# The second layer's modulation, summed over row blocks on VectorE

## The chip, the cores and the metric

The kernel runs on one core of a Trainium2 chip. The metric is the device time of one execution in microseconds, the median of several runs. A profile is one further execution, recorded by the hardware profiler.

## What is computed

The reference is a trunk of two layers over 512 latent tokens and 256 context tokens, 1024 wide. In each layer six vectors of 1024 numbers, the modulation, scale, shift and gate the tokens:

```
for l in range(DEPTH):                          # DEPTH = 2
    ctx_out = l < DEPTH - 1
    mod_l = (silu_c @ w_mod[l] + b_mod[l])      # for the latent tokens
    mod_c = (silu_cc @ w_mod[l] + b_mod[l])     # for the context tokens
    sh_m, sc_m, gt_m, sh_f, sc_f, gt_f = split(mod, 6)   # for l and for c
    hl = rmsnorm(xl, g_pre_mix) * (1 + sc_ml) + sh_ml    # hc likewise
    y_c, y_l = token_mixing(hc @ w_in, hl @ w_in, ...)   # S5, neighbourhood, GLA, windowed heads
    xl = xl + gt_ml * rmsnorm(y_l @ w_out, g_post_mix)
    hl = rmsnorm(xl, g_pre_ffn) * (1 + sc_fl) + sh_fl
    xl = xl + gt_fl * rmsnorm(conv_ffn(hl, w_up, conv_w, w_down), g_post_ffn)
    if ctx_out: the same two updates for the context tokens xc
return xl
```

`w_mod[l]` has 1024 rows and 6144 columns, so that one layer's modulation reads 25 MB for two vectors (one for each kind of token). In the last layer only `sh_m` and `sc_m` are needed for the context, since its other outputs are not.

## The kernel before, in words

Channels lie on partitions, 8 tiles of 128 (`KT = 8`), tokens along the free axis. Large products are made of three matmuls each (high and low parts of both operands, `split`, L243): ScalarE makes the high part of a weight tile or of an activation, VectorE the low one.

**The modulation.** `silu_c` (L166) leaves `cT`: for each of the 8 tiles of channels 32 columns, of which the first two are the two streams (latent and context) and the rest zero. A round of `mod_round` (L180) makes 2048 of the 6144 columns. It goes over 32 blocks of `w_mod`, 128 rows by 512 columns and 256 KB each, loaded by SP into three buffers of the tag `wm`. Each block is multiplied on TensorE by `cT` in four matmuls, one for each 128 columns, which write the four groups of 32 partitions of one PSUM tile `modp` and accumulate over the 8 tiles of channels; as the operands are float32, each matmul is two instructions, so a block is eight. At the end of a round VectorE copies the PSUM tile (`modrow`), TensorE turns it in four transposes (`modt`), and VectorE adds the bias and makes the factors that the layer uses. The first round of layer 0 is made by another function (`mod_first`, L1633).

**When a round is made.** Rounds are generators, one step a block. They wait in the list `later`, and `pump(n)` (L1296) takes n steps. In the mixing of a layer `gap` (L487) calls pump at each gap between units of attention, GLA or S5; in the feed-forward stage `ffn` (L1571) calls it once after each f from 2 on, with n = 4 (`KN['pump']`, L1582). Layer 0's mixing makes rounds 1 and 2 of layer 0; layer 0's feed-forward stage makes rounds 0 and 1 of layer 1 (`L1748`); layer 1's mixing makes round 2 of layer 1 (`mods`, L1374 and L1424), from the GLA stage on.

**The feed-forward stage.** There are 22 f, blocks of 128 hidden channels in groups of 6, 6, 6 and 4. For each f, `dense` (L434, its matmuls at L442) makes gate and value of 512 latent and 256 context tokens: four PSUM tiles, of the tags `m` (four buffers), `d` and `o` (two each; `modp` holds one `o` during a round, and transposes of the S5 build take `o` too). `ffn_hidden` (L1536) turns them into `hid`: ScalarE scales the gate (L1546), VectorE adds the two neighbours (L1547, L1548), ScalarE applies gelu (L1549), VectorE multiplies by the value (L1550), and the result is split (L245, L246). After a group `row_product` (L275, its matmuls at L283) multiplies it by `w_down`. The first two f of the stage are made together by `dense4` (L457, matmuls at L480).

**The S5 build.** `s5_build` (L574) makes the S5 operators of a layer: layer 0's during the start of layer 0, layer 1's in layer 0's feed-forward stage, one step after each f from 5 on (L1583). It runs mostly on VectorE in small operations (`E`, L624 to L639, and `bl`, `cl`, L699 to L714), with transposes and small products on TensorE (L721, L734), and stores to DRAM from POOL's queue. Its tiles lie in the pool `bp`.

**The order.** The program is traced in the order described and a planner (a list scheduler with a simulated timeline) orders the instructions of each engine: the earlier an instruction is traced the higher its priority, those of weight loads (L415) are raised, and an instruction that is ready earlier than one of higher priority goes ahead of it. On the chip each engine then keeps that order. Loads of weights and of `w_mod` blocks are issued by SP in one queue.

Of the kernel before, what the change touches and what calls it, by code (L numbers as in the profile page):

```python
# [10 lines left out]
FT = mybir.dt.float32  # L11
# [5 lines left out]
OP = mybir.AluOpType  # L17
# [6 lines left out]
KT = 8  # L24
# [9 lines left out]
EPS = 1e-6  # L34

RATES = ((2, 0, 2), (1, 0, 2))
KN = dict(build=(1, 1, 1, 2, 1, 1, 1, 1, 2, 1, 1), build1=0, r00=2, r01=1, r02=2, r10=0, r11=3, r12=1, glaA=1, glaB=1, s5=2, s5b=2, na1=0, na2=1, sw1=1, sw2=2, swA=4, pump=4, rows=2, d4=2, ahead=3000, s5n=3, gt=2, six=1, bg=1, wat=(0, 2, 4, 6), wmb=5, go0=12, s5e=4, modg0=0, modg1=0, mod1=1, resA=1, resB=0, slow=1, slow0=5, ro1=2, ro2=2)
NEG = -1e30


# [45 lines left out]
class Trunk:  # L86
# [79 lines left out]
    def silu_c(self):  # L166
# [10 lines left out]
        nc.vector.tensor_copy(self.cT[:, :, 0], p[:, 0:8])  # L177
        nc.vector.tensor_copy(self.cT[:, :, 1], p[:, 32:40])

    def mod_round(self, l, r, pool, tag="o"):  # L180


        nc, L = self.nc, self.L[l]
        if r == 0:
            L["mod"] = self.cst.tile([128, 2, 48], FT, name=f"mod{l}")
        p = self.ps("modp", tag)
        for i in range(4 * KT):
            k, c = i // 4, i % 4
            w = pool.tile([128, 512], FT, name="wm", tag="wm", bufs=3)
            nc.sync.dma_start(w, self.a["w_mod"][l, 128 * k:128 * (k + 1), 2048 * r + 512 * c:2048 * r + 512 * c + 512])  # L190
            for j in range(4):

                nc.tensor.matmul(p[32 * j:32 * j + 32, 128 * c:128 * c + 128], self.cT[:, k, :], w[:, 128 * j:128 * j + 128],  # L193
                                 start=(i == 0), stop=(k == KT - 1), skip_group_check=True)
            yield
        row = pool.tile([128, 512], FT, name="modrow", tag="wm", bufs=3)
        nc.vector.tensor_copy(row, p)
        t = self.ps("modt", tag)
        for b in range(4):
            nc.tensor.transpose(t[:, 128 * b:128 * (b + 1)], row[:, 128 * b:128 * (b + 1)], self.ident)  # L200
        tv = t.rearrange("p (b j s) -> p s b j", b=4, j=4)
        bj = lambda v: v.rearrange("p (b j) -> p b j", b=4)
        for s in range(2):
            nc.vector.tensor_tensor(bj(L["mod"][:, s, 16 * r:16 * r + 16]), tv[:, s], bj(L["va"][:, 16 * r:16 * r + 16]), op=OP.add)
        va = L["va"]
        bc = lambda v: v[:, None, :].to_broadcast([128, 2, 8])
        if r == 0:
            L["Am"] = self.cst.tile([128, 2, 8], FT, name=f"Am{l}")
            nc.vector.scalar_tensor_tensor(L["Am"], L["mod"][:, :, 8:16], 1.0, bc(va[:, 48:56]), op0=OP.add, op1=OP.mult)
        if r == 1:  # L210
            L["Gm"] = self.cst.tile([128, 2, 8], FT, name=f"Gm{l}")
            nc.vector.tensor_tensor(L["Gm"], L["mod"][:, :, 16:24], bc(va[:, 56:64]), op=OP.mult)
        if r == 2:
            L["Af"] = self.cst.tile([128, 2, 8], FT, name=f"Af{l}")
            nc.vector.scalar_tensor_tensor(L["Af"], L["mod"][:, :, 32:40], 1.0, bc(va[:, 64:72]), op0=OP.add, op1=OP.mult)
            L["Gf"] = self.cst.tile([128, 2, 8], FT, name=f"Gf{l}")
            nc.vector.tensor_tensor(L["Gf"], L["mod"][:, :, 40:48], bc(va[:, 72:80]), op=OP.mult)
# [356 lines left out]
    def s5_build(self, l):  # L574

        nc, a, L = self.nc, self.a, self.L[l]
# [13 lines left out]
        k, r, cs, sn = T("thk"), T("thr"), T("cs"), T("sn")  # L590
# [27 lines left out]
        for i in range(3):  # L618
            s = [ph[:, i, 0], ph[:, i, 1]]
# [1 line left out]

        L["s5"] = self.dr.tile([8, 128, S_ALL], FT, name=f"s5ops{l}")
        for q in range(2):
            E = [self.bp.tile([128, 8, 96], FT, name=f"E{i}", tag=f"E{i}") for i in (0, 1)]  # L624
            w = 1
            for i in (0, 1):
                nc.vector.tensor_copy(E[i][:, :, 0], ph[:, 3, i, 8 * q:8 * q + 8])
            while w < 96:
                m = min(w, 96 - w)
# [4 lines left out]
            for i, x in enumerate((E[1], E[0], E[1])):  # L634
                if i == 2:
                    nc.vector.tensor_scalar(x, x, -1.0, None, op0=OP.mult)
                for g in range(2):
                    c = S_ROT + 288 * g + 96 * i
# [33 lines left out]
        for i, nm in enumerate(("s5_c_re", "s5_c_im")):  # L672
            for q in range(2):
# [3 lines left out]
                p = self.ps("cps", "o")  # L677
# [17 lines left out]
        nc.vector.tensor_copy(pC[:, :, 8], p4[:, :, 0])  # L695
        yield

        kk = self.bp.tile([128, 8, 8, 16], FT, name="kk")
        for r in range(8):  # L699
            bl, cl = (self.bp.tile([128, 2, 2, n, 16], FT, name=nm, tag=nm, bufs=2 - l) for nm, n in (("bl", 8), ("cl", 9)))  # L700
            for g in range(2):
                c = 2 * r + g
                for x, pt, n, o, planes in ((Bb, pB, 8, bl, ((0, 1), (3, -3))), (Cm, pC, 9, cl, ((0, 3), (3, -1)))):

                    t = []
# [11 lines left out]
            p = self.ps("btp", "o")  # L717
            for g in range(2):
                for i in range(2):
                    o = 128 * (2 * g + i)  # L720
# [6 lines left out]
            p = self.ps("toe", "o")  # L727
# [579 lines left out]
    def mixing(self, l, H, ctx_out):  # L1307

        nc, a = self.nc, self.a
# [61 lines left out]
        self.fill += later[i:]  # L1371
        yp.append(self.open(f"wm{l}", "left"))
        self.wm = yp[-1][1]
        mods = lambda: self.later.append(self.chain([self.mod_round(l, r, self.wm, "m" if KN[f"modg{l}"] else "o") for r in ((1, 2) if l == 0 else (2,) if KN["mod1"] else ())]))  # L1374
        if KN[f"modg{l}"]:
            mods()
        self.rate = KN[f"r{l}0"]
        S = {}

# [40 lines left out]


        self.rate = KN[f"r{l}1"]
        if not KN[f"modg{l}"]:
            mods()  # L1424
        ph = phase("s5")
        outputs("s", (0, 1))
        zd = [self.dr.tile([128, 8, 96], FT, name=f"s5zd{l}{t}") for t in range(2)]
# [281 lines left out]
    def run(self):  # L1709
# [27 lines left out]
        for l in range(DEPTH):  # L1737
# [7 lines left out]
            if ctx_out:  # L1745
                bp = self.open("s5b1", "right")
                self.bp = bp[1]
                self.later = [self.chain([self.mod_round(1, r, self.wm) for r in ((0, 1) if KN['mod1'] else (0, 1, 2))])]  # L1748
                self.slow = self.s5_build(1)

            def last():
# [68 lines left out]
```

## Time and profile before

| | before |
|---|---|
| median of 3 runs | 1958.98 us (1958.47 to 1961.07) |
| profiled execution | 1961.94 us |
| its span | 1960.2 us |
| TensorE busy | 1824.7 us, 93% |
| VectorE busy | 1093.3 us, 56% |
| ScalarE busy | 720.5 us, 37% |
| POOL busy | 158.3 us, 8% |
| mean granted TensorE clock | 0.953 |

All times are on the span's own axis, from 0 to 1960.2 us. PE is TensorE's matmul side, PEld its weight loads, DVE VectorE, ACT ScalarE, POOL GpSimd, SP the engine that issues most DMAs. Matmuls are pipelined, so a row's duration (0.39 us for 512 columns) is longer than the distance to the next start (0.23); starts are what to compare. A granted clock of 1.00 is 2.4 GHz, 0.50 is 1.2 GHz.

### The profile page before, as it was taken

The page shows a single profiled execution, that of the slowest core. Times are in us where ns is not written, and L with a number is a line of the kernel's source. Part 1 is how long each engine was busy: PE and PEld are TensorE (multiplying, and loading weights), DVE is VectorE, ACT ScalarE, POOL GpSimd, SP SyncE. Part 2 cuts the span into 40 slices and gives each one's busy share as a digit, 9 for nine tenths or more (in the row PEclk, how much of TensorE's full clock was granted, in tenths as well). Part 3 has the DMA queues.
Part 4 walks back from the last instruction along what each step waited for, and adds up shares of the span by engine and source line. Part 5 has one row for each costly group of instructions (what it writes and reads, how often), then busy time and mean ns, then how long its engine had stood idle before and what let it go on. Part 6 is the DMA issues. An engine that isn't in the chain of part 4 may idle for free.

```text
span 1960.2 us, 31588 instructions
## 1 busy us (share of the span) xinstructions
PE 1824.7 (93%) x12345; PEld 1485.0 (76%) x12345; DVE 1093.3 (56%) x2665; ACT 720.5 (37%) x1481; POOL 158.3 (8%) x233
## 2 busy tenths in 40 slices
PE   4899989798998999999999997999898989999997
PEld 2888768465678888888888877877676688888885
DVE  5796655653778614644533475666564654444446
ACT  4334312533654223212321245631354543333332
POOL 5121000100111100000000020000100100000001
PEclk8999889798998999999999998999898999999998
DMA  9254146444123424333442223247522033323232
GB/s 300 60 172 128 39 128 187 114 132 133 62 87 105 151 65 121 119 113 103 124 135 80 66 79 129 81 124 231 143 57 88 23 104 122 109 84 111 83 111 83
DMA packets 243188, 219.85 MB, mean 112 GB/s; under 512 B 45324, under 2 KB 187590, under 8 KB 243040
## 3 DMA queue, kind: packets, MB, share of 16 engines
q1 hardware_dynamic: 225600, 198.52, 32.7%
q0 software_dynamic: 6528, 15.06, 2.7%
q10 hardware_dynamic: 10912, 4.26, 1.4%
q8 instruction: 97, 1.59, 0.3%
q14 instruction: 51, 0.42, 0.1%
HBM read 190.27 MB, written 27.53 MB: 111 GB/s over the span
## 4 chain that ended last, share of the span: by engine, by line
PE 80%; DMA 6%; DVE 6%; ACT 3%; issue 1%; ACTq 1%; POOL 1%; SPq 1%; DVEq 0%; POOLq 0%
PE pd L442 28%; PE pd L283 19%; PE pd L453 12%; PE pd L480 3%; DMA wm<-in_w_mod_dram 3%; PE modp L193 2%; PE pd4c L480 1%; DMA nawide<-in_rpb_pad_dram 1%; PE s5o L853 1%; PE nao L1018 1%; PE go L1248 1%; ACTq L950 1%; PE swo L1133 1%; POOL natab L954 1%; DVE wlo L246 1%
## 5 line engine op out<-in xcount | busy, mean ns | idle before, releaser
L246 DVE TENSOR_TENSOR wlo<-wst,whi 128x1024 fp32r<-128x1024 f32 x190 | 232.8, 1226 | 286.8 <-ACT whi L245 281.5
L245 ACT CAST whi<-wst 128x1024 fp32r<-128x1024 f32 x190 | 199.4, 1050 | 435.5 <-PE pd L283 122.4
L283 PE MATMUL pd<-whi,hidh 128*128 128x512 f32 x440 | 172.1, 392 | 1.7 <-DVE za L323 1.6
L283 PE MATMUL pd<-whi,hidl 128*128 128x512 f32 x440 | 171.9, 391 | 0.0
L283 PE MATMUL pd<-wlo,hidh 128*128 128x512 f32 x440 | 170.7, 390 | 0.0
L283 PEld LDWEIGHTS pd<-whi,hidh 128*128 128x128 f32 x440 | 82.6, 188 | 21.1 <-DVE za L323 2.9
L283 PEld LDWEIGHTS pd<-whi,hidl 128*128 128x128 f32 x440 | 82.6, 188 | 17.7 <-issue 0.6
L283 PEld LDWEIGHTS pd<-wlo,hidh 128*128 128x128 f32 x440 | 82.6, 188 | 17.4
L1550 DVE TENSOR_TENSOR fg<-fg,pd 128x512 f32<-128x512 f32 x64 | 38.6, 604 | 92.1 <-PE pd L442 91.3
L193 PE MATMUL modp<-wm,cT 128*32 128x128 f32 x1280 | 60.8, 295 | 24.9 <-DMA wm<-in_w_mod_dram 21.2
L1549 ACT ACTIVATE fg<-fg 128x512 f32<-128x512 f32 x66 | 36.8, 560 | 107.5 <-DVE fg L1548 103.8
L193 PEld LDWEIGHTS modp<-wm,cT 128*32 128x32 f32 x1280 | 31.2, 112 | 50.9 <-DMA wm<-in_w_mod_dram 29.6
L1547 DVE SCALAR_TENSOR_TENSOR fg<-pd,vb,fg 128x511 f32<-128x511 f32 x64 | 42.3, 662 | 38.0 <-ACT fg L1546 37.8
L1600 DVE TENSOR_TENSOR za<-za,pd 128x512 f32<-128x512 f32 (+1 forms) x40 | 21.9, 552 | 71.1 <-PE pd L283 71.0
L1546 ACT ACTIVATE fg<-pd,vb 128x512 f32<-128x512 f32 x64 | 39.4, 618 | 57.1 <-PE pd L442 56.9
L245 ACT CAST hidh<-fg 128x512 fp32r<-128x512 f32 x66 | 35.9, 547 | 46.8 <-DVE fg L1550 46.7
L334 POOL TENSOR_TENSOR za<-za,g 128x768 f32<-128x768 f32 x10 | 18.8, 1882 | 419.1 <-ACT sq L324 388.1
L442 PE MATMUL pd<-h0h,whi 128*128 128x512 f32 (+1 forms) x118 | 43.8, 372 | 4.7 <-DVE fg L1548 2.9
L246 DVE TENSOR_TENSOR hidl<-fg,hidh 128x512 fp32r<-128x512 f32 x66 | 39.4, 599 | 11.1 <-ACT hidh L245 11.0
L1548 DVE SCALAR_TENSOR_TENSOR fg<-pd,vb,fg 128x511 f32<-128x511 f32 x64 | 42.5, 665 | 1.6
L442 PE MATMUL pd<-h2l,whi 128*128 128x512 f32 (+1 forms) x118 | 42.6, 361 | 0.0
L442 PE MATMUL pd<-h0l,whi 128*128 128x512 f32 (+1 forms) x118 | 42.4, 360 | 0.0
(685 smaller groups left out, 5193.4 us busy)
## 6 DMA issues: line engine op xcount, KB each, us to landing
wst<-in_ffn_w_up_dram SPq DMA_DIRECT2D x88, 512.0 KB
wm<-in_w_mod_dram SPq DMA_DIRECT2D x160, 256.0 KB
wst<-in_ffn_w_down_dram SPq DMA_DIRECT2D x44, 512.0 KB
wst<-in_w_in_dram SPq DMA_DIRECT2D x36, 512.0 KB
pka<-s5ops SPq DMA_DIRECT2D x16, 544.0 KB
wm<-in_w_mod_dram SPq DMA_DIRECT2D x16, 512.0 KB
wst<-in_w_out_dram SPq DMA_DIRECT2D x12, 512.0 KB
xres<-za SPq DMA_DIRECT2D x16, 384.0 KB
```

The source lines that it names most:

```text
L193: nc.tensor.matmul(p[32 * j:32 * j + 32, 128 * c:128 * c + 128], self.cT[:, k, :], w[:, 128 * j:128 * j + 128], start=(i == 0), stop=(k == ...
L245: nc.scalar.copy(hi, src)
L246: return nc.vector.tensor_tensor(lo, src, hi.bitcast(FT), op=OP.subtract)
L283: self.nc.tensor.matmul(o, ht[:, sl], wp[:, i, :], start=j == 0 and x == 0, stop=j == n - 1 and x == 2)
L442: nc.tensor.matmul(o, wt[:, j, ms], ht[:, c0:c0 + cn], start=j == 0 and i == 0, stop=j == len(ks) - 1 and i == 2)
L453: nc.tensor.matmul(o, wt[:, j, ms], ht[:, c0:c0 + cn], start=j == 0 and i == 0, stop=j == len(ks) - 1 and i == 2)
L480: self.nc.tensor.matmul(o, wt[:, k, :], ht[:, sl], start=(first and k == 0 and x == 0), stop=(k == KT - 1 and x == 2), skip_group_check=True)
L1546: nc.scalar.mul(g, p, cw(1))
L1547: nc.vector.scalar_tensor_tensor(g[:, 1:cn], p[:, 0:cn - 1], cw(0), g[:, 1:cn], op0=OP.mult, op1=OP.add)
L1548: nc.vector.scalar_tensor_tensor(g[:, 0:cn - 1], p[:, 1:cn], cw(2), g[:, 0:cn - 1], op0=OP.mult, op1=OP.add)
L1549: nc.scalar.activation(g, g, AF.Gelu_apprx_tanh)
L1550: nc.vector.tensor_tensor(g, g, p2, op=OP.mult)
```

## The change

All three rounds of layer 1's modulation are traced in layer 0's feed-forward stage, six blocks a call of `pump` instead of four, and none in layer 1's mixing. They are made by a new function, `mod_sums`. It goes over the four groups of 512 columns of a round; for each it loads the 8 blocks of 128 rows and sums them on VectorE, each row weighted by its channel's factor (a per-partition scalar out of `cT`): one multiply for the first block, one multiply-add for each further one, into one accumulator for each stream. Round 0 is made for both streams, rounds 1 and 2 for the latent stream alone. Then TensorE sums the accumulator over its 128 partitions: a stationary operand `ones` with a single column of ones (column s for stream s), four matmuls for each accumulator, into the same PSUM layout as before. The end of a round is the old code, in a function of its own (`mod_end`), which layer 0's rounds use too.

To make room in the pool, `E0` and `E1` become one tile `E`, and `kk` uses the same single buffer.

```diff
+    def mod_sums(self, r, streams, pool, tag="o"):
+        nc, L = self.nc, self.L[1]
+        if r == 0:
+            L["mod"] = self.cst.tile([128, 2, 48], FT, name="mod1")
+        p = self.ps("modp", tag)
+        for c in range(4):
+            acc = [self.bp.tile([128, 512], FT, name=f"macc{s}", tag=f"macc{s}", bufs=1) for s in range(streams)]
+            for k in range(KT):
+                w = pool.tile([128, 512], FT, name="wm", tag="wm", bufs=3)
+                nc.sync.dma_start(w, self.a["w_mod"][1, 128 * k:128 * (k + 1), 2048 * r + 512 * c:2048 * r + 512 * c + 512])
+                for s, o in enumerate(acc):
+                    if k == 0:
+                        nc.vector.tensor_scalar(o, w, self.cT[:, k, s:s + 1], None, op0=OP.mult)
+                    else:
+                        nc.vector.scalar_tensor_tensor(o, w, self.cT[:, k, s:s + 1], o, op0=OP.mult, op1=OP.add)
+                yield
+            for s, o in enumerate(acc):
+                for j in range(4):
+                    nc.tensor.matmul(p[32 * j:32 * j + 32, 128 * c:128 * c + 128], self.ones[:, s], o[:, 128 * j:128 * j + 128],
+                                     start=(c + s == 0), stop=(s == streams - 1), skip_group_check=True)
+        self.mod_end(1, r, p, pool, tag)
...
-            E = [self.bp.tile([128, 8, 96], FT, name=f"E{i}", tag=f"E{i}") for i in (0, 1)]
+            E = self.bp.tile([128, 2, 8, 96], FT, name="E", tag="E", bufs=1)
+            E = [E[:, i] for i in (0, 1)]
...
-        kk = self.bp.tile([128, 8, 8, 16], FT, name="kk")
+        kk = self.bp.tile([128, 2, 8, 96], FT, name="kk", tag="E", bufs=1).rearrange("p a b c -> p (a b c)")[:, 0:1024]
...
-        mods = lambda: self.later.append(self.chain([self.mod_round(l, r, self.wm, "m" if KN[f"modg{l}"] else "o") for r in ((1, 2) if l == 0 else (2,) if KN["mod1"] else ())]))
+        mods = lambda: self.later.extend([self.chain([self.mod_round(0, r, self.wm) for r in (1, 2)])] if l == 0 else [])
...
-                self.later = [self.chain([self.mod_round(1, r, self.wm) for r in ((0, 1) if KN['mod1'] else (0, 1, 2))])]
+
+                self.ones = self.bp.tile([128, 2, 32], FT, name="ones")
+                nc.gpsimd.memset(self.ones, 0.0)
+                for s in range(2):
+                    nc.gpsimd.memset(self.ones[:, s, s:s + 1], 1.0)
+                self.later = [self.chain([self.mod_sums(r, 2 if r == 0 else 1, self.wm) for r in range(3)])]
```

In `KN`, `pump=4` becomes `pump=6`, and the names `modg0`, `modg1` and `mod1` go.

## Rows read from the trace of the kernel before

**Rows 1.** The page: busy us, share of the span and instructions of each engine.
```profile
PE 1824.7 (93%) x12345; PEld 1485.0 (76%) x12345; DVE 1093.3 (56%) x2665; ACT 720.5 (37%) x1481; POOL 158.3 (8%) x233
```
**Rows 2.** Two stretches: length, busy us (instructions) by engine, clock, DMA, GB/s.
```profile
607.00:1068.00 461.00, 455.35 (x2937) 381.93 (x2936) 220.34 (x467) 124.11 (x196) 23.68 (x36) 0.99 0.36 111
1303.00:1394.00 91.00, 90.99 (x931) 72.69 (x926) 53.59 (x113) 17.84 (x32) 0.52 (x1) 1.00 0.65 198
```
**Rows 3.** Stretches again, line L193 alone: PE and PEld only.
```profile
607.00:1068.00 461.00, 21.46 (x512) 12.24 (x512) 0.99 0.36 111
1303.00:1394.00 91.00, 10.05 (x240) 6.02 (x240) 1.00 0.65 198
```
**Rows 4.** Chain of waits, feed-forward stage of layer 0: start, us, what.
```profile
755.08 0.79 PE modp L193 x24
...
773.30 0.79 PE modp L193 x24
...
831.97 0.44 PE modt L200 x4
...
904.21 16.65 PE pd L442 x96
```
**Rows 5.** Timeline of TensorE around a group of 8: start, us, what.
```profile
761.38 0.28 PE L442 MATMUL pd<-h0h,whi 128*128 128x256 f32 x1
761.59 0.43 PE L193 MATMUL modp<-wm,cT 128*32 128x128 f32 x8
...
762.17 0.28 PE L442 MATMUL pd<-h0h,wlo 128*128 128x256 f32 x1
762.29 0.28 PE L442 MATMUL pd<-h1h,whi 128*128 128x256 f32 x1
```
**Rows 6.** The first call: timelines of TensorE and VectorE, and two stretches.
```profile
610.39 0.86 PE L193 MATMUL modp<-wm,cT 128*32 128x128 f32 x24
616.31 0.58 PE L442 MATMUL pd<-h0h,wlo 128*128 128x256 f32 x1
614.66 0.74 DVE L1548 SCALAR_TENSOR_TENSOR fg<-pd,vb,fg 128x511 f32<-128x511 f32 x1
610.00:616.00 6.00, 2.18 (x42) 1.25 (x42) 5.93 (x18) 2.06 (x3) 0.00 (x0) 0.61 0.67 219
616.00:621.00 5.00, 5.00 (x30) 4.69 (x23) 3.12 (x9) 2.32 (x4) 0.00 (x0) 0.50 0.99 295
```
**Rows 7.** Groups by shape on VectorE: count, busy us, mean ns, idle before.
```profile
L1007 DVE TENSOR_SCALAR nass<-nass,su 128x512 f32<-128x512 f32 x32 | 15.7, 490 | 0.8
L241 DVE SCALAR_TENSOR_TENSOR grs<-ru,r 128x512 f32<-128x512 f32 x4 | 2.8, 690 | 0.1
```
**Rows 8.** Waits, 607 to 1068 us: TensorE's, SP's; total us, times, longest.
```profile
PE modp L193 <- DMA wm<-in_w_mod_dram: 3.8, 2, 3.1
SPq L190 <- PE modp L193: 132.5, 32, 6.5
```
**Rows 9.** Timelines of TensorE and VectorE where the first down product starts.
```profile
688.59 0.50 PE L283 MATMUL pd<-whi,hidh 128*128 128x512 f32 x1
690.00 0.42 DVE L246 TENSOR_TENSOR hidl<-fg,hidh 128x256 fp32r<-128x256 f32 x1
```
**Rows 10.** Timeline of VectorE in layer 1's S5 stage and behind it.
```profile
1368.33 0.95 DVE L830 TENSOR_TENSOR s5x<-bu,pka 128x768 f32<-128x768 f32 x1
1372.68 0.95 DVE L830 TENSOR_TENSOR s5x<-bu,pka 128x768 f32<-128x768 f32 x1
1393.53 1.54 DVE L971 COPY nvw<-nv 128x256 f32<-128x256 f32 x6 [8.00 <-DMA s5zd<-s5zz]
```
**Rows 11.** Layer 0's build: timelines of POOL and ScalarE; page's DMA issues (us to landing).
```profile
116.73 1.49 POOL L639 DMA_DIRECT2D s5ops<-E  x2 [1.13 <-DVE E L636]
119.21 0.27 ACT L738 COPY kk<-toe 128x128 f32<-128x128 f32 x1 [0.69 <-PE toe L737]
s5ops<-E POOLq DMA_DIRECT2D x24, 192.0 KB, 3.1
```

More of the change, by code (lines that the diff above doesn't have):

```diff
@@ L36 @@
 RATES = ((2, 0, 2), (1, 0, 2))
-KN = dict(build=(1, 1, 1, 2, 1, 1, 1, 1, 2, 1, 1), build1=0, r00=2, r01=1, r02=2, r10=0, r11=3, r12=1, glaA=1, glaB=1, s5=2, s5b=2, na1=0, na2=1, sw1=1, sw2=2, swA=4, pump=4, rows=2, d4=2, ahead=3000, s5n=3, gt=2, six=1, bg=1, wat=(0, 2, 4, 6), wmb=5, go0=12, s5e=4, modg0=0, modg1=0, mod1=1, resA=1, resB=0, slow=1, slow0=5, ro1=2, ro2=2)
+KN = dict(build=(1, 1, 1, 2, 1, 1, 1, 1, 2, 1, 1), build1=0, r00=2, r01=1, r02=2, r10=0, r11=3, r12=1, glaA=1, glaB=1, s5=2, s5b=2, na1=0, na2=1, sw1=1, sw2=2, swA=4, pump=6, rows=2, d4=2, ahead=3000, s5n=3, gt=2, six=1, bg=1, wat=(0, 2, 4, 6), wmb=5, go0=12, s5e=4, resA=1, resB=0, slow=1, slow0=5, ro1=2, ro2=2)
 NEG = -1e30
@@ L195, in mod_round, with mod_end @@
             yield
+        self.mod_end(l, r, p, pool, tag)
+    def mod_end(self, l, r, p, pool, tag):
+        nc, L = self.nc, self.L[l]
         row = pool.tile([128, 512], FT, name="modrow", tag="wm", bufs=3)
@@ L696, in s5_build @@
         yield
-        kk = self.bp.tile([128, 8, 8, 16], FT, name="kk")
+        kk = self.bp.tile([128, 2, 8, 96], FT, name="kk", tag="E", bufs=1).rearrange("p a b c -> p (a b c)")[:, 0:1024]
+        kk = kk.rearrange("p (r t c) -> p r t c", r=8, t=8)
         for r in range(8):
@@ L1373, in mixing @@
         self.wm = yp[-1][1]
-        mods = lambda: self.later.append(self.chain([self.mod_round(l, r, self.wm, "m" if KN[f"modg{l}"] else "o") for r in ((1, 2) if l == 0 else (2,) if KN["mod1"] else ())]))
-        if KN[f"modg{l}"]:
-            mods()
+        mods = lambda: self.later.extend([self.chain([self.mod_round(0, r, self.wm) for r in (1, 2)])] if l == 0 else [])
         self.rate = KN[f"r{l}0"]
@@ L1422, in mixing @@
         self.rate = KN[f"r{l}1"]
-        if not KN[f"modg{l}"]:
-            mods()
+        mods()
         ph = phase("s5")
```

## The prediction

> **What bounds the kernel now.** I read the page's busy line first: TensorE is busy for 93% of the span, VectorE for 56% [rows 1]. The profiled execution took 1961.94 us, of which the span is 1960.2; it lies 3.0 us above the median of the runs (1958.98), so I make the sum against 1961.94 and take the same difference off the median. Then the stretches that the change touches, engine by engine. In layer 0's feed-forward stage (607 to 1068 us) TensorE is busy 455.35 of 461 us, at a granted clock of 0.99, and VectorE 220.34. In layer 1's mixing the old sums lie between 1312 and 1401 us; from 1303 to 1394 TensorE is busy 90.99 of 91 us and VectorE 53.59 [rows 2]. The same stretches for the old line alone (L193) give what it holds of TensorE: 21.46 us and 10.05 us [rows 3]. The chain of waits in the feed-forward stage runs on TensorE from piece to piece, so what is taken from it there comes off the end.
>
> **What is removed in the feed-forward stage.** Before, 64 blocks of w_mod (2 rounds) go through TensorE there, four at each of 16 calls of pump, eight instructions a block (512 in rows 3, divided by 64). The price of a call is read from the chain: one f without a call lasts 16.65 us, and from one group of 24 to the next is 773.30 - 755.08 = 18.22 us [rows 4]. So a call costs 1.57 us. Part of it is the group of 8 that comes alone: from 761.38 to 762.17 there are 0.79 us, in which two 256-column matmuls at 0.12 (762.17 to 762.29) belong to the dense product, so the 8 cost 0.55 us and the 24 cost 1.02 [rows 4, 5]. Fifteen calls: 23.6 us.
>
> The first call is dearer. TensorE enters it at 610.39 and goes on with dense work at 616.31, having waited for blocks [rows 6, 8], and from 616 to 621 the granted clock is 0.50, the lower of its levels (1.2 GHz), so 5 us of work cost 2.5 too many: 8.4 us in all [rows 6]. Without the call TensorE would run through its 24 matmuls of 256 columns by 613.3 and then want the PSUM tile that L1548 gives back at 615.4 [rows 6]: 2.1 us of a new wait, gain 6.3. But VectorE is busy 5.93 of the 6 us from 610 to 616 [rows 6]; three blocks of the first round there (two sums each, 1.4 us a block) would put L1548 back by 4.1 us and leave 2. I take 4.
>
> **What is added there.** 96 blocks at six a call are again 16 calls. TensorE gets 12 groups. Round 0 has two streams, four times 16 instructions, priced between the 8 and the 24 at 0.79: 3.2 us. Rounds 1 and 2 have four groups of 8 each, at 0.55: 4.4 us. The third round's end adds its transposes, 0.44 [rows 4] and 0.2 of disturbance. Together 8.2 us.
>
> VectorE gets 128 operations of 128x512: 112 with two tensor operands, priced by a row of this shape with SBUF operands, 690 ns, and 16 plain multiplies at 490 ns [rows 7]. That is 77.3 + 7.8 = 85.1 us, to 305 of some 442 us: it lies beside the dense products. If that cover were gone it would be the 85 us themselves.
>
> Each group on TensorE is a new wait on VectorE; behind it in TensorE's queue stand the dense matmuls. From below a group costs nothing, from above it comes two sums late, 12 times 1.4 = 17 us. I take 0: transposes of the S5 build wait on VectorE in the same way in this stretch, and TensorE's whole idle time in it is 5.65 us [rows 2]. Each sum waits on VectorE for its DMA; behind it stand the operations on fg and the splits. At the end of the first group of f's the last hidl is ready at 690.42, and TensorE, which starts the down product at 688.59, reads it as its seventeenth matmul, at 692.3: 1.9 us of slack [rows 9]. Three such ends, 0 to 4 us together; I take 0. The single accumulator makes the next first multiply wait for TensorE's read; the 137 us that VectorE has left hide that, else it adds to the same bound.
>
> SP issues 32 blocks more in this stage, and none in layer 1's. It already stands 132.5 us there waiting for block buffers [rows 8], with the ffn weights behind those waits; now VectorE frees them. 0, as long as VectorE is not late.
>
> **What is removed in layer 1.** 10.05 us of TensorE, and for ten groups of 24 about 0.23 us of disturbance each (1.02 less 0.79): 12.4 us, with 2 or 3 us of waiting for the last blocks 15. All of it would come off if TensorE alone set this stretch. It does not: S5 units follow each other on VectorE 4.35 us apart (1368.33, 1372.68), and the neighbourhood stage starts only when the last unit's result has gone out, at 1393.53 [rows 10]. Where the units set the pace, less work on TensorE only lets projections come earlier, which pays later if at all. Bounds 0 and 15; I take 7.
>
> **E and kk in one buffer.** In layer 0's build the last E transfers are issued by 118.22 and land 3.1 us later, kk's first copy is at 119.21 [rows 11]: ScalarE may wait 2.1 us there once. kk is only stored for the S5 stage; 0, at most 2.1. The `memset`s of `ones` run on POOL, busy 23.68 of 461 us [rows 2]: 0.
>
> **Sum.** 23.6 + 4 - 8.2 + 7 = 26.4 us. 1961.94 becomes 1935.5, and by the median 1958.98 becomes 1932.6: I say 1932.
>
> **A rule weighed.** TensorE's busy share may flatter it: weight loads are busy only 381.93 of the 461 us [rows 2]. The Trainium skill says so (Perfetto Trace Analysis, section Identifying the Most-Contended Engine): matmul busy time is no good measure of how near the engine is to its limit, the busy share of weight loads is. By that measure a sixth of the stage is room. The 1.57 us by which a call lengthens an f speak against it; the sum that it would give is the third rival's.
>
> **The rivals.**
> 1. Layer 1 gives nothing, as its S5 units set the pace: 23.6 + 4 - 8.2 = 19.4, so 1940. For it: the 4.35 us spacing. Against: TensorE has no idle time from 1303 to 1394.
> 2. Layer 1 gives all 15, the start 6.3: 36.7, so 1922. For it: the same full TensorE. Against: the start lies in VectorE's fullest stretch.
> 3. TensorE has room between its matmuls, and only weight loads count: 12.24 us removed [rows 3], a quarter (128 of 512) added back, 4 at the start, half of 6.02 in layer 1: 16, so 1943. Against: dense matmuls keep a steady pitch.
> 4. Slower: VectorE, which takes its instructions in order, stands before blocks that have not landed, and the fg chain stands behind. Its place is calls 1 to 16. TensorE's two waits for blocks there were 3.8 us, 1.9 each [rows 8]. If all 96 blocks cost VectorE that, it needs 220 + 85 + 182 = 487 us for a stage of 442: 45 us more, less the 26.4, so 1978. It begins to lengthen the stage at (442 - 305) / 96 = 1.4 us a block and makes the kernel slower from 1.7. For it: six blocks a call through three buffers. Against: 62 of the 64 blocks before came without a wait, and other ready work can stand ahead of a sum.
> 5. It does not do what it says: the gain is given back one to one in new waits (12 of 2.2 us). 1959.
>
> **How the numbers follow.** Chances: the forecast 0.52 (its own range 1924 to 1939), rival 1 0.13, rival 2 0.10, rival 3 0.07, rival 4 0.14, rival 5 0.04. A measurement of this kernel tells 0.2%, 3.9 us, from no change. Faster by more: 0.52 + 0.13 + 0.10 + 0.07 = 0.82; within it 0.04; slower 0.14. The range takes in rivals 1 to 3 and part of the late groups (17 us, which alone would give 1949): 1916 to 1950.
>
> **What would show it.** L193 gone from layer 1, and in the feed-forward stage 128 instructions of the new line, in 12 groups; an f with no group at 16.65 us plus the S5 build's share; VectorE near 305 us in the stage, its waits for w blocks under 1 us each; 1303 to 1394 shorter by about 7 us, with VectorE's S5 units as close as before. The forecast is wrong if TensorE waits for the accumulators by more than 1 us a group, if dense products start behind late hidl or late weights, or if layer 1's stretch keeps its length.

## The result and the profile after

The changed kernel takes 1930.35 us (median of 4 runs, 1927.51 to 1932.73); beside it the kernel before took 1960.03. The ratio is 0.9848, 95% interval 0.9831 to 0.9865: 29.7 us, or 1.5%, faster. I had predicted 1932. The sum was nearly right; of its terms, several were not. Lines have moved: the old loop's L193 is now L218, the sums are L194 and L196, the matmul that adds over partitions is L201, the dense product of the feed-forward stage is L471 (was L442), and the low parts of weights and activations are made at L275 (was L246).

The page's busy line of the changed kernel answers to [rows 1]: TensorE has 640 matmuls and 34 us less, VectorE 128 operations and 74 us more.

```profile
PE 1790.8 (93%) x11705; PEld 1465.3 (76%) x11705; DVE 1167.0 (61%) x2793; ACT 727.1 (38%) x1486; POOL 157.3 (8%) x236
```

To see where the time went I cut both traces at the same instructions: the first dense product of layer 0's feed-forward stage (f = 2), the first product of its last group (f = 18), and the end. In us, with a second profiled execution of each kernel:

| | up to f = 2 | f = 2 to f = 18 | f = 18 to the end | span |
|---|---|---|---|---|
| before | 610.0 | 458.7 | 891.5 | 1960.2 |
| before, second | 610.7 | 457.2 | 890.3 | 1958.3 |
| after | 601.0 | 442.3 | 884.4 | 1927.7 |
| after, second | 603.0 | 442.3 | 881.2 | 1926.5 |
| difference, after less before (first executions) | -9.0 | -16.4 | -7.1 | -32.5 |
| predicted | 0 | -19.4 | -7 | -26.4 |

The stage itself gave less than I said, layer 1 what I said, and 9 us came ahead of the stage, where I had nothing.

Stretches of the changed kernel (columns as in [rows 2]): the stage, five us at its start and the five behind them. Granted clock is the third number from the end.

```profile
599.00:1043.00 444.00, 437.64 (x2546) 371.84 (x2548) 297.11 (x624) 122.32 (x196) 23.69 (x36) 0.99 0.43 131
601.00:606.00 5.00, 0.53 (x2) 0.27 (x2) 5.00 (x9) 0.51 (x1) 0.00 (x0) 0.53 0.68 206
606.00:611.00 5.00, 4.94 (x23) 4.94 (x24) 5.00 (x10) 3.88 (x5) 0.00 (x0) 0.50 0.58 180
```

VectorE is at 297.11 of 444 us (I had said 305), TensorE idles 6.4 us (5.65 before). The same stage with L201 alone, PE and PEld: it answers to [rows 3].

```profile
599.00:1043.00 444.00, 6.05 (x124) 2.56 (x128) 0.99 0.43 131
```

The chain of waits there (start, us, what) answers to [rows 4]. A group of 16 is a piece of 0.57 us and a group of 8 one of 0.36 (the time between starts, which is what a group costs, is longer: see the account of the prediction), and an f without a group lasts 16.65 us, as before.

```profile
606.06 35.79 PE pd L471 x190
641.85 0.57 PE modp L201 x16
...
726.10 16.65 PE pd L471 x96
742.75 0.57 PE modp L201 x16
...
885.50 16.65 PE pd L471 x96
902.15 0.35 PE modp L201 x8
...
1042.99 0.36 PE modp L201 x8
...
1049.38 0.44 PE modt L229 x4
```

No accumulator comes late. These are all the waits of TensorE in the stage (total us, times, longest us):

```profile
PE pd L471 <- DVE wlo L275: 4.5, 1, 4.5
PE pd L471 <- ACT whi L274: 1.8, 1, 1.8
```

The sums on VectorE as a group (columns as in [rows 7]): they take 748 ns where I took 690.

```profile
L196 DVE SCALAR_TENSOR_TENSOR macc<-wm,cT,macc 128x512 f32<-128x512 f32 x112 | 82.3, 748 | 19.6 <-DMA wm<-in_w_mod_dram 18.9
```

What they waited for in the stage (total us, times, longest us):

```profile
DVE macc L196 <- DMA wm<-in_w_mod_dram: 18.0, 13, 4.2
```

The start of the stage is where the result is worse than I said. The timeline of TensorE (start, us, operation, idle time before it and what ended it) answers to [rows 6].

```profile
600.98 0.39 PE L471 MATMUL pd<-h0h,whi 128*128 128x256 f32 x1 [1.82 <-ACT whi L274]
601.20 0.33 PE L471 MATMUL pd<-h0l,whi 128*128 128x256 f32 x1
606.06 0.58 PE L471 MATMUL pd<-h0h,wlo 128*128 128x256 f32 x1 [4.53 <-DVE wlo L275]
```

The timeline of VectorE ahead of it:

```profile
596.31 1.42 DVE L196 SCALAR_TENSOR_TENSOR macc<-wm,cT,macc 128x512 f32<-128x512 f32 x2 [0.81 <-DMA wm<-in_w_mod_dram]
...
602.34 0.75 DVE L196 SCALAR_TENSOR_TENSOR macc<-wm,cT,macc 128x512 f32<-128x512 f32 x1
...
603.74 0.75 DVE L196 SCALAR_TENSOR_TENSOR macc<-wm,cT,macc 128x512 f32<-128x512 f32 x1
...
604.79 1.22 DVE L275 TENSOR_TENSOR wlo<-wst,whi 128x1024 fp32r<-128x1024 f32 x1
```

TensorE no longer waits for blocks; it waits for the low part of its weights (wlo), which stands on VectorE behind sums. From the first dense product to the next steady run it was 610.0 to 616.3 before and is 601.0 to 606.1 now: 1.3 us won, not 4. Then the granted clock is 0.50, its lower level (1.2 GHz), for 5 us, as before. The wait of 1.8 us ahead of the first dense product stands in the kernel before too.

### The profile page after: what moved, and what is told of

Same layout as the page of the kernel before. It is cut to its first block, busy times and chain, and to the rows that moved or that the text cites. A ratio compares the mean times of both kernels' runs of the same rounds, so it can differ in the third digit from the quotient of the medians.

```text
span 1927.7 us, 30566 instructions
## 1 busy us (share of the span) xinstructions
PE 1790.8 (93%) x11705; PEld 1465.3 (76%) x11705; DVE 1167.0 (61%) x2793; ACT 727.1 (38%) x1486; POOL 157.3 (8%) x236
## 4 chain that ended last, share of the span: by engine, by line
PE 78%; DVE 8%; DMA 7%; ACT 3%; issue 2%; SPq 1%; POOL 1%; ACTq 0%; DVEq 0%; POOLq 0%
PE pd L471 28%; PE pd L312 20%; PE pd L482 12%; DMA wm<-in_w_mod_dram 3%; PE pd L509 2%; PE nao L1049 1%; DVE wlo L275 1%; PE swo L1164 1%; PE go L1279 1%; DMA nawide<-in_rpb_pad_dram 1%; DMA pka<-s5ops 1%; PE s5o L884 1%; PE go L1282 1%; PE swpt L1152 1%; PE napt L1043 1%
## 5 line engine op out<-in xcount | busy, mean ns | idle before, releaser
L275 DVE TENSOR_TENSOR wlo<-wst,whi 128x1024 fp32r<-128x1024 f32 x190 | 232.9, 1226 | 247.5 <-ACT whi L274 236.6
L196 DVE SCALAR_TENSOR_TENSOR macc<-wm,cT,macc 128x512 f32<-128x512 f32 x112 | 82.3, 748 | 19.6 <-DMA wm<-in_w_mod_dram 18.9
L1574 ACT ACTIVATE fg<-pd,vb 128x512 f32<-128x512 f32 x64 | 39.4, 618 | 46.0 <-PE pd L471 46.0
L274 ACT CAST hidh<-fg 128x512 fp32r<-128x512 f32 x66 | 36.1, 547 | 36.5 <-DVE fg L1578 36.1
L471 PE MATMUL pd<-h0h,whi 128*128 128x512 f32 (+1 forms) x118 | 43.7, 370 | 4.7 <-DVE fg L1576 2.9
L471 PE MATMUL pd<-h0h,wlo 128*128 128x512 f32 (+1 forms) x118 | 42.4, 359 | 4.5 <-DVE wlo L275 4.5
L275 DVE TENSOR_TENSOR hidl<-fg,hidh 128x512 fp32r<-128x512 f32 x66 | 39.2, 597 | 7.0 <-ACT hidh L274 6.9
L218 PE MATMUL modp<-wm,cT 128*32 128x128 f32 x512 | 28.9, 313 | 14.9 <-DMA wm<-in_w_mod_dram 12.8
L471 PE MATMUL pd<-h1h,whi 128*128 128x512 f32 (+1 forms) x118 | 42.4, 360 | 0.0
```

Source lines behind the costliest of these rows:

```text
L196: nc.vector.scalar_tensor_tensor(o, w, self.cT[:, k, s:s + 1], o, op0=OP.mult, op1=OP.add)
L274: nc.scalar.copy(hi, src)
L275: return nc.vector.tensor_tensor(lo, src, hi.bitcast(FT), op=OP.subtract)
L471: nc.tensor.matmul(o, wt[:, j, ms], ht[:, c0:c0 + cn], start=j == 0 and i == 0, stop=j == len(ks) - 1 and i == 2)
L1574: nc.scalar.mul(g, p, cw(1))
```

## The experiments

All runs in one table; stretches in us from the profiled execution of each. A profiled execution can lie far from its kernel's median (unshare0's two were 9.1 and 10.6 us over it), so "up to f = 2" of one execution is to be taken with care, while the stage's length repeats within 2 us.

| run | median, us | ratio to before, 95% | up to f = 2 | f = 2 to 18 | f = 18 to end |
|---|---|---|---|---|---|
| share0 | 1956.55 | 0.9973 (0.9959 to 0.9987) | 609.2 | 458.9 | 887.8 |
| unshare0 | 1930.73 | 0.9856 (0.9829 to 0.9883) | 613.8 | 441.3 | 882.9 |
| unshare0b | 1928.7 | 0.9837 (0.9818 to 0.9856) | 614.7 | 443.0 | 879.9 |
| move | 1955.8 | 0.9971 (0.9961 to 0.998) | 605.0 | 468.3 | 880.9 |
| sums2 | 1928.24 | 0.9844 (0.9824 to 0.9863) | 601.9 | 439.1 | 880.7 |
| after2 | 1930.0 | 0.9838 (0.9815 to 0.986) | 603.0 | 442.3 | 881.2 |
| before2 | 1960.04, one run | | 610.7 | 457.2 | 890.3 |
| late | 1925.4 | 0.9822 (0.9798 to 0.9846) | 606.4 | 442.5 | 881.0 |
| dbl | 1928.94 | 0.9828 (0.9801 to 0.9854) | 611.7 | 442.8 | 876.5 |
| hold | 1927.2 | 0.9842 (0.9821 to 0.9863) | 603.3 | 439.6 | 879.6 |
| hold2 | 1926.18 | 0.9828 (0.9811 to 0.9845) | 607.4 | 436.8 | 885.0 |
| drop1 | 1948.39 | 0.994 (0.9925 to 0.9955) | 608.2 | 457.0 | 880.0 |

**Move alone, without the sums (move).** The changed kernel with the old loop in place of the sums:

```
-self.chain([self.mod_sums(r, 2 if r == 0 else 1, self.wm) for r in range(3)])
+self.chain([self.mod_round(1, r, self.wm) for r in range(3)])
```

> The changed kernel with all three rounds moved to the feed-forward stage as it has them, six blocks a call, but multiplied on TensorE with the old loop in place of the sums on VectorE. 384 instructions of the old line in that stage in place of 128 on partial sums. By the prices of my prediction the 96 blocks take 96 x 0.39 = 37.7 us there in place of the new 8.2, so 29.5 us more than the changed kernel, and layer 1 keeps its 7: about 1960, level with the kernel before (9 us of that from the shared buffer if theory A holds, spent on the third round's 12.6). Rival C (only weight loads count, TensorE has room between its matmuls): 256 more instructions cost about 6 us, so about 1937. Rival D (the sums cost VectorE and through it the fg chain as much as TensorE wins): level with the changed kernel, 1930.

It takes 1955.8 us (1960 was expected), some 25 us more than the changed kernel, and its stage is 26.0 us longer (468.3 against 442.3). So nearly the whole gain is the sums', and not the move's. The stage with the old loop's line alone, in this kernel (PE, then PEld):

```profile
605.00:1073.00 468.00, 31.96 (x768) 19.40 (x768) 0.99 0.41 127
```

The line has 768 instructions there, not the expected 384, as each matmul is two. Its matmul busy time is 31.96 us, that of L201 in the changed kernel 6.05: 25.9 us less, and the stage is 26.0 shorter. That the two agree so closely is in part chance. Counted by the starts of TensorE's matmuls (how, is shown in the account of the prediction), the groups of the old line cost 35.9 us in this stage and those of the sums 8.1: 27.8 less. The changed kernel gives 1.8 of that back at the start of the stage, where TensorE waits 4.5 us for wlo and here only 1.1. Rival C (1937) and rival D (1930) fall. The expected price of an old block, 0.39 us, is near: by starts it is 0.38, where the busy time alone (31.96 / 96) says 0.33. Weight loads differ by 16.8 us (19.40 - 2.56). The Trainium skill (Perfetto Trace Analysis, section Identifying the Most-Contended Engine) names MFU (the share of peak arithmetic) and the busy share of weight loads, in place of matmul busy time, as measures of how near TensorE is to its limit. Taken as the price of what leaves the engine, which is rival C's reading and not what the page says, the busy share of weight loads would give 16.8 us here; this trace, with 26.0, does not agree with that reading.

**Does VectorE have room? (dbl).** A second sum that nobody reads, in rounds 1 and 2:

```
-acc = [... for s in range(streams)]
+acc = [... for s in range(2)]
...
-for s, o in enumerate(acc):          # the matmuls
+for s, o in enumerate(acc[:streams]):
```

> The changed kernel with a second sum, which nobody reads, beside the one of rounds 1 and 2: 64 more operations of 128x512 on VectorE, 64 x 0.74 = 47 us, to about 345 of 442 us of the stage. Theory A (the sums lie beside the dense products with room to spare): dense start to last group 442 to 444 us, about 1931. Rival H (the sums stand before the operations on fg and the splits, so that more of them lengthens the stage, my rival 4 with its own price): a tenth to a half of the 47 us comes through, 447 to 465 us, 1935 or more.

Its median is 1928.94 and its stage 442.8 us, 0.5 more. In this stretch, cut as the one of the changed kernel above, VectorE is at 334 us in place of 297:

```profile
609.70:1054.50 444.80, 438.28 (x2550) 371.87 (x2549) 333.72 (x688) 121.81 (x196) 23.69 (x36) 0.99 0.43 131
```

Theory A holds and rival H falls: 37 us more of VectorE in the stage cost nothing that this can measure. (I had expected 47 by single durations; part of the difference is that sums that follow each other overlap, two take 1.41 to 1.42 us.) The sums do lie beside the dense products.

**The stop at the start (late, hold).** In late no blocks are asked for in the first call, and seven instead of six in the others:

```
-self.pump(KN['pump'])
+self.pump(7 if f > 2 else 0)
```

> The changed kernel with no blocks in the first call of pump (f = 2) and seven instead of six in the others. TensorE stood 4.53 us there for the weights' low part (wlo), which VectorE made only after two sums that waited for their blocks. Theory A (the late blocks in VectorE's queue are that stall): the first dense product goes on after 1 to 2 us (the PSUM tile that my prediction put there), dense start to last group 439 us in place of 442.3, about 1927. Rival G (VectorE and the weights' loads are late there anyway, as in the kernel before): the stall stays at 4 to 5 us, 442, about 1930.

The stop stayed (1.8 + 4.6 us) and the stage too (442.5), but this decides nothing between the theories: the program's planner had put the first sums ahead of wlo all the same (they start 7 us ahead of the first dense product, as in the changed kernel). So the edit did not do what it was for. Its median is 1925.4, and the intervals of late and after2 overlap. In hold each call's blocks are tied behind the last split of the f before:

```
-self.split(g, hi[:, c0:c0 + cn], lo[:, c0:c0 + cn])
+self.hl = self.split(g, hi[:, c0:c0 + cn], lo[:, c0:c0 + cn])
...
-self.pump(KN['pump'])
+with self.tc.issue_after(self.hl.ins):
+    self.pump(KN['pump'])
```

> The changed kernel with each call's blocks tied behind the last split of the f before it (issue_after on the operation that writes hidl), so that no sum can stand on VectorE ahead of the first dense product's weights: in the run called late the planner had put the first sums there all the same, and TensorE stood 4.6 us as before. Theory A (the sums that wait for blocks ahead of wlo and fg are the stop at the start of the stage): the stop falls from 1.8 + 4.5 us to 2 to 3 us, dense start to last group from 442.3 to 438 to 440, time about 4 us under the changed kernel's, 1926. Rival G (fg and the weights are late there by themselves): stop and stretch stay, 442, 1930. Rival I (the held sums pile up and the last calls' groups come late at the end of the stage): stretch 444 or more, 1932 or more.

TensorE's timeline in hold, where the changed kernel has 4.53:

```profile
603.33 0.38 PE L471 MATMUL pd<-h0h,whi 128*128 128x256 f32 x1 [1.83 <-ACT whi L274]
...
606.39 0.58 PE L471 MATMUL pd<-h0h,wlo 128*128 128x256 f32 x1 [2.56 <-DVE wlo L275]
```

The wait falls by 2.0 us and the stage by 2.7 (442.3 to 439.6, as expected). Theory A holds in part: of the 4.53 us the sums ahead of wlo are a little under half. The stop as a whole is still 1.8 + 2.6 us, where 2 to 3 were expected; VectorE, with no sum ahead of wlo, is still busy there without a gap, on fg and on the S5 build, and what the rest of the stop hangs on was not tried. The median, 1927.2, can't be told from the changed kernel's 1930.0: the expected 4 us were too many, and 2.7 lie within the scatter of the runs.

**Round 2: what its place in layer 1 costs (sums2, hold2, drop1).** sums2 sums rounds 0 and 1 only and leaves round 2 in layer 1's mixing; hold2 is that with the tie of hold.

```
-KN = dict(... pump=6 ...)
+KN = dict(... pump=4 ...)
-self.later = [self.chain([self.mod_sums(... for r in range(3)])]
+self.later = [self.chain([self.mod_sums(... for r in range(2)])]
-[self.mod_round(0, r, self.wm) for r in (1, 2)])] if l == 0 else []
+[self.mod_round(l, r, self.wm) for r in ((1, 2) if l == 0 else (2,))])]
```

> The changed kernel with only rounds 0 and 1 summed on VectorE in the feed-forward stage (four blocks a call), and round 2 left in layer 1's mixing with the old loop, as in the kernel before. Theory A: layer 1's stretch loses its 7.5 us again, and the stage saves one round's groups and end (2.2 + 0.6 = 2.8 us): about 4.7 us slower than the changed kernel, 1935. Rival E (layer 1's S5 units set the pace and the round there costs nothing; what layer 1 gains comes from elsewhere): about 2.8 us faster than the changed kernel, 1927. Rival F (all of TensorE's 10 us and the last wait count): about 12 us slower, 1942.

> The same tie in the kernel that sums rounds 0 and 1 only and leaves round 2 in layer 1's mixing (the run called sums2: 439.1 us from dense start to last group, 1928). Theory A: 435 to 436 us, about 1924 to 1925. Rival G: 439, 1928.

The stage is 3.2 us shorter than the changed kernel's in sums2 (2.8 expected), and 2.8 in hold2 against hold. Layer 1 does not get longer for it: 880.7 and 885.0 us from f = 18 to the end, where the changed kernel has 884.4 and 881.2. In total 1928.24 and 1926.18: theory A's 1935 and rival F's 1942 fall, and the numbers are rival E's. But its reason is not: drop1 is the kernel before without round 2 of layer 1 in any place.

```
-for r in ((1, 2) if l == 0 else (2,) if KN["mod1"] else ())
+for r in ((1, 2) if l == 0 else ())
...
+if l == 1 and r == 0:
+    nc.vector.memset(L["mod"][:, :, 32:48], 0.0)
-if r == 2:
+if r == 2 or (l == 1 and r == 0):
```

> The kernel before without round 2 of layer 1 in any place (its shift, scale and gate are taken as zero), layer 0 and the feed-forward stage as they were. Theory A (the round holds up layer 1's stretch between the gated part's last norm and the first product of the neighbourhood attention, 93.7 us in the kernel before and 93.6 in its second execution, 86.8 and 85.8 in the changed kernel): 86 us there and about 7 us off the whole, 1953. Rival E (the S5 units set the pace there and the round is hidden, as the run called sums2, which keeps the round, has only 89.3 us there and is as fast as the changed kernel): 92 to 94 us, 1960. Rival F (all that TensorE does for the round comes off): 79 us, 1947.

It is 11.9 us faster than the kernel before (8.8 to 14.7 by the interval), with layer 1 at 880.0 us (890.9 in the mean of the two executions of before): the round does cost there, some 11 us in this built program, between theory A's 7 and rival F's 13. From the last norm of the gated part (gms) to the first product of the neighbourhood attention it is 82.9 us, before 93.7 and 93.6, after 86.8 and 85.8, sums2 89.3. Over all fourteen executions it is 89.3 to 93.7 us in the five with the round in it and 82.9 to 88.0 in the nine without. These stretches in the kernel before, after and in drop1, one fence each:

```profile
1334.00:1428.00 94.00, 85.32 (x688) 68.10 (x688) 59.16 (x125) 25.82 (x50) 8.44 (x9) 0.91 0.67 182
```

```profile
1311.00:1398.00 87.00, 71.52 (x475) 59.06 (x473) 53.91 (x120) 25.27 (x46) 6.75 (x9) 0.88 0.52 134
```

```profile
1334.00:1417.00 83.00, 70.82 (x473) 58.61 (x471) 53.43 (x120) 24.95 (x45) 6.67 (x9) 0.90 0.55 141
```

After and drop1 do the same work there, 71.5 and 70.8 us of TensorE, in 87 and 83 us. TensorE idles 8.7 us of this stretch before, 15.5 after and 12.2 in drop1: of 13.8 us of TensorE work that left, 7 came off, and the rest turned into idle time. What it then waits for, in the changed kernel (us, times, longest), are copies on ScalarE and VectorE ahead of the attention:

```profile
PE nvp L1014 <- ACT navw L1009: 6.0, 1, 6.0
PE pd L482 <- ACT sk L797: 3.0, 1, 3.0
PE nvp L1008 <- DVE nvw L1002: 2.9, 1, 2.9
```

drop1 takes out the round's work on TensorE and its loads together (182 GB/s in this stretch before, 141 in drop1), so which of the two holds the stretch up is not separated. sums2 and hold2 pay for the round in this stretch (89.3 and 89.9 us); where they earn it back, so that layer 1 as a whole is short, is open. Part of it is no matter of the round: from the last window-attention product (swo) to the next feed-forward stage's first dense product it is 59.9 and 59.2 us in the kernel before and 60.0 in share0, but 55.2 to 57.3 in the other eleven executions, drop1 among them. I did not find what that stretch hangs on.

**The 9 us ahead of the stage (share0, unshare0, unshare0b, after2, before2).** Only the buffer that E and kk share is new there. share0 is the kernel before with it in layer 0 alone, unshare0 the changed kernel without it in layer 0:

```
-E = [self.bp.tile([128, 8, 96], FT, name=f"E{i}", tag=f"E{i}") for i in (0, 1)]
+if l == 0: (unshare0: l == 1)
+    E = self.bp.tile([128, 2, 8, 96], FT, name="E", tag="E", bufs=1)
+    E = [E[:, i] for i in (0, 1)]
+else:
+    E = [self.bp.tile([128, 8, 96], FT, name=f"E{i}", tag=f"E{i}") for i in (0, 1)]
... and kk likewise
```

> The kernel before, with E and kk in one buffer in layer 0's S5 build alone (layer 1 keeps its own); modulation untouched. Theory A: the 9.0 us by which the changed kernel comes earlier to the feed-forward stage of layer 0 (first dense product at 609.96 before, 600.98 after) come from this shared buffer, which orders the S5 build in layer 0's mixing otherwise: this kernel reaches that product at about 601 and takes 9 us less than the kernel before, about 1951. Rival B: the shared buffer costs or gives nothing (my prediction: 0, at most 2.1 lost), and the 9 us come from another order of the whole program or are scatter between two executions: first dense product at about 610, time within 2 us of the kernel before, about 1960.

> The changed kernel with the old E and kk buffers back in layer 0 (shared in layer 1 alone). Theory A (the shared buffer gives the 9 us before the feed-forward stage): first dense product at about 610, 9 us slower than the changed kernel, about 1939, 21 us faster than the kernel before. Rival B: first dense product at about 601 and about 1930, as the changed kernel.

> The changed kernel once more, for a second profiled execution and as the base of the runs beside it. Theory A (the 9.0 us before the feed-forward stage belong to the changed kernel's order): first dense product of layer 0's feed-forward stage at 601 within 2 us again. Rival B (a good part is scatter between executions): 604 to 610. Both: 442 us from that product to the first of the last group of f (442.3 in the first execution), about 1930.

> The kernel before once more, for a second profiled execution. Theory A: first dense product of the feed-forward stage at 610 within 2 us. Rival B: 602 to 607 or beyond 613. Both: 458.6 us from there to the last group of f.

> The changed kernel with separate E and kk buffers in layer 0 once more: its first profiled execution was 9 us above its own median, so where it stood at the feed-forward stage says little. Six kernels with the shared buffer in layer 0 reach the first norm of the gated part (gms) at 213.3 to 218.1 us, the two executions of the kernel before at 221.5 and 220.8. Theory A (the shared buffer gives about 5 us in layer 0's mixing, as the run called share0 has it by its median): gms at 220 to 222, first dense product at 608 to 611, time about 5 us over the changed kernel's, 1935. Rival B (it gives 5 us up to gms, which later waits in layer 0's mixing take back): gms at 220 to 222, first dense product at 601 to 605, 1930.

By its median share0 is 5.1 us faster than the kernel before (2.5 to 8.0 by the interval): the buffer gives something, though not theory A's 9 us, and the stage starts at 609.2 and not at 601. In its trace only 0.8 of 4.3 us lie ahead of the stage, where the buffer is; 3.8 lie behind f = 18, where nothing was changed. In the changed kernel, though, taking it out lost nothing (1930.73 and 1928.7 against 1930.35 and 1930.0), so theory A does not hold there, and by the medians rival B's numbers do; the first dense product, at 613.8 and 614.7 us in executions 9 to 11 us over the median, is at neither theory's place. Nor does the trace bind the gain to the buffer. With it, TensorE's instructions ahead of the stage stand in another order in layer 0's S5 build, and the first gms comes at 213.3 to 218.1 us in the nine executions with it, at 220.4 to 221.5 in four of the five without; but drop1 has the old buffers and the same TensorE order up to layer 1 as the kernel before, and reaches gms at 217.1.

The two repeats came within 0.7 and 2.0 us of the first executions, so this is less scatter between executions than a difference between built programs: after, move, sums2 and dbl, whose TensorE order up to the stage is the same, reach it at 601.0, 605.0, 601.9 and 611.7 us. The largest steps between after and dbl lie in layer 0's S5 stage: between 277 and 310 us (of the changed kernel) dbl's lag grows from 0.6 to 7.2 us. TensorE's waits from bu's start to the attention, first in the changed kernel, then in dbl:

```profile
PE nas L1028 <- DVE nass L1034: 4.2, 1, 4.2
PE bu L853 <- DMA pka<-s5ops: 1.5, 1, 1.5
```

```profile
PE bu L853 <- DMA pka<-s5ops: 6.3, 3, 3.4
PE nas L1028 <- DVE nass L1034: 5.3, 1, 5.3
```

There the loads of the S5 operands land later in one built program than in another that has the same code for them, which is 4.8 of the 10.7 us. They are not the whole of it: sums2 waits 4.6 us for the same loads and reaches the stage at 601.9. What sets their landing I have not tried. So the 9 us are left without a shown cause; up to 5 of them may be the shared buffer's, and they are not the modulation's.

No version was shown to beat the changed kernel: late, hold, hold2, sums2 and dbl lie at 1925 to 1929, and the intervals of all of them overlap its own.

## Why the prediction was right, step by step

The stage is taken apart by the starts of TensorE's matmuls. Behind a matmul of 512 columns the next one starts 0.227 us later, behind one of 256 columns 0.120; these steady steps of the dense and down products make 413.6 us of the stage in either kernel. What the starts lie further apart is put down to what stands between them, the step behind a group included:

| us between starts, beyond the steady steps | before | after | difference |
|---|---|---|---|
| first 12 us of the stage (the first call; before, one block of the second too) | 8.53 | 7.39 | -1.14 |
| groups of the modulation (L193, now L201) | 22.65 | 8.10 | -14.55 |
| transposes at a round's end | 0.80 | 0.87 | +0.07 |
| the S5 build's matmuls | 12.56 | 12.07 | -0.49 |
| dense steps longer than steady | 0.55 | 0.28 | -0.27 |
| sum | 45.09 | 28.71 | -16.38 |

- **Calls removed, 23.6 us: right.** A group of 24 and a group of 8 in the kernel before, and a group of 8 in the changed kernel:

```profile
754.80 0.28 PE L442 MATMUL pd<-h7h,wlo 128*128 128x256 f32 x1
755.01 0.86 PE L193 MATMUL modp<-wm,cT 128*32 128x128 f32 x24
755.80 0.50 PE L442 MATMUL pd<-h0h,whi 128*128 128x512 f32 x1
756.14 0.39 PE L442 MATMUL pd<-h0l,whi 128*128 128x512 f32 x1
...
761.95 0.39 PE L442 MATMUL pd<-h0l,whi 128*128 128x256 f32 x1
```

```profile
760.03 0.39 PE L471 MATMUL pd<-h0h,whi 128*128 128x512 f32 x1
760.36 0.43 PE L201 MATMUL modp<-macc,ones 128*32 128x128 f32 x8
760.71 0.50 PE L471 MATMUL pd<-h0l,whi 128*128 128x512 f32 x1
761.04 0.39 PE L471 MATMUL pd<-h0h,wlo 128*128 128x512 f32 x1
```

  From 754.80 to 755.80 is 1.00 us, 0.88 more than a steady step, and the step behind it (to 756.14) is 0.11 longer than steady; with the 8 (761.38 to 761.95 to 762.17, the outer two in [rows 5]) at 0.45 and 0.10 the call costs 1.54 us, against 1.57 in the sum. Over the stage, 59 blocks behind its first 12 us cost 22.65 us, which is 23.0 for fifteen calls. The line's busy time (21.46 / 16 = 1.34 a call [rows 3]) would have been too little, since it leaves out the longer step.
- **First call, +4: about 1. This is the term of the stage that was mis-sized.** The bounds were 2 to 6.3, and it is under both: 1.3 us up to the steady run, and 0.8 over the first 12 us (1.14 less the 0.38 of a block of the second call). In the second executions the stop gave 1.3 us too, but nothing is left of it after 12 us: from 616 to 621 us the granted clock was 0.70 in that execution of the kernel before, against 0.50 in the first [rows 6]. I had put up to three blocks on VectorE there and charged them with delaying L1548 and its PSUM tile. What they delay is wlo, the next weights, which I did not look at. It is the place where rival 4's mechanism happens: VectorE stands before blocks or works through sums, and TensorE's weights stand behind. Dense products behind late weights were one of my signs that the forecast is wrong, and at this place the sign is there. It stays at this place; 13 waits of VectorE for blocks, 18.0 us together, the longest 4.2, cost nothing elsewhere, though I had said under 1 us each.
- **Added groups, -8.2: right, 8.1 in the stage.** A group of 8 costs 0.45 and 0.10 in the step behind it, the 0.55 of the sum. The third round's transposes, 0.44, come behind f = 18 and so outside this stretch. So the first call alone lacks about 3 us of its 4, as much as the stage lacks of 19.4 in all; what else differs is under 1 us each way and balances.
- **Sums on VectorE, 85.1 us hidden: right in kind.** One by one they take 90.1 (82.3 for 112 and 7.8 for 16): a sum with a scalar from each partition costs 748 ns, as the fg operations of the same form in the kernel before had shown (746 and 748); I took a row with an immediate scalar. That the scalar makes the difference is read from these rows and was not tried. 0 on the path: dbl shows it. The wait for accumulators at 0: TensorE shows none of size in the stage.
- **Layer 1, 7 of 0 to 15: the size was right, the reason not.** It gave 7.1 and 9.2 us. I had taken S5 units 4.35 us apart for the pace of this stretch, from two neighbouring starts [rows 10]. The eight units lie 3.6 to 8.4 us apart; these are their first and last, before and after (timelines of VectorE):

```profile
1339.50 0.96 DVE L830 TENSOR_TENSOR s5x<-bu,pka 128x768 f32<-128x768 f32 x1
...
1378.75 0.96 DVE L830 TENSOR_TENSOR s5x<-bu,pka 128x768 f32<-128x768 f32 x1 [0.68 <-PE bu L822]
```

```profile
1318.13 0.96 DVE L861 TENSOR_TENSOR s5x<-bu,pka 128x768 f32<-128x768 f32 x1
...
1354.63 0.95 DVE L861 TENSOR_TENSOR s5x<-bu,pka 128x768 f32<-128x768 f32 x1
```

  From first to last it is 39.3 us before and 36.5 after; 39.2 to 39.4 in all five executions with the round there, sums2 and hold2 among them, and 34.5 to 37.9 in the nine without (34.8 in drop1). So the units do not set a pace of their own: the round holds them up. It did cost 11 in the kernel before (drop1). That the removal gave 7 is still not only the round's doing, since layer 1 as a whole is as short in sums2, which has it.
- **E and kk in one buffer, 0: not shown to be right.** By itself in the kernel before it gave 5 us, though its trace does not show them at the buffer.
- **The rivals.** Rival 1 (layer 1 gives nothing) falls with drop1; rival 2's 15 is not reached; rival 3 falls with move; rival 4 is true at one place, at the price of some 2 us (hold), and does not decide; rival 5's waits do not exist.

So 26.4 of the predicted sum stand against 29.7 measured by the medians and 32.5 in the traces. That the sum is so near is in part luck: the 3 us lacking at the first call are outweighed by 8 to 9 us ahead of the stage for which I had no term and found no cause.

## What to carry to other kernels

Where TensorE is full, price what leaves it by the starts of its matmuls: from the last one before a group to the first behind it, less a steady step, and what the next step is longer. Busy time gave less here (1.34 us for a call that cost 1.54). Before moving work to an engine with half of its time free, look at the one place where that engine is full, and at who stands behind it there. The planner here put new work at that place on its own, though the program asked for it one call later (late); a tie to a later instruction kept it out (hold). A pace read from two neighbouring starts may be one of many: read the whole row of them. Compare two built programs by stretches cut at the same instructions: a difference of a few us ahead of the change may come from how the program was built anew.

## What the runs showed of the hardware

- A 128x512 sum of two tensors on VectorE with a scalar for each partition takes 748 ns in these sums; the row with an immediate scalar took 690 [rows 7], and a plain multiply takes 482 (median).
- Between dense matmuls a group of 8 instructions with a 32-column weight and 128 columns costs TensorE 0.45 us and a group of 24 0.88, by starts, and the dense step behind the group is 0.10 to 0.11 us longer than steady.
- Built programs with the same TensorE order up to a point reach it up to 10 us apart (601.0 and 611.7), each repeatably where it was repeated (0.7 to 2.0 us); 4.8 us of that are longer waits for loads of S5 operands.
